# First feed-forward's end: where the residual rows of token tiles 4 to 7 are kept

## The chip, the cores and the metric

The program runs on one core of a Trainium2 chip. The metric is its time on the device in microseconds (us), from start to end of one execution, as the median of several runs. A core has five engines, each of which works through its own row of instructions in order: TensorE (PE, matrix products), VectorE (DVE), ScalarE (ACT), GpSimd (POOL) and SyncE (SP), which here only issues transfers. An instruction waits until what it reads has been written and until the buffer that it writes is no longer read, and all that stands behind it on its engine waits with it.

## The reference

One layer of a trunk over 1024 tokens of 1024 channels, in float32:

```python
x = x + 0.5 * rms_norm((silu(rms_norm(x) @ Wg) * (rms_norm(x) @ Wu)) @ W_out)   # first feed-forward, 2816 wide
u = rms_norm(x)
rq, rk, rv, rg, nq, nk, nv, g_ret, g_na = split(u @ w_mix_in)                   # one combined projection
y_ret = (silu(rg) * head_norm(forward + backward retention)) @ w_ret_out
y_na = neighbourhood_attention(nq, nk, nv, bias) @ w_na_out
x = x + rms_norm((sigmoid(g_ret) * y_ret + sigmoid(g_na) * y_na) @ w_mix_out)
x = x + 0.5 * rms_norm(second feed-forward of rms_norm(x))
```

Every norm has a gain of its own. The change lies where the first of these lines ends and the second and third begin.

## The kernel before, in words

**Products.** Each float32 product is made from operands split into a high and a low part (`wh` and `wl` for a block of weights): ACT rounds the high part (L61), DVE subtracts to get the low part (L62), and three matmuls, high by high (L88), high by low (L89) and low by high (L90), are summed in a bank of PSUM (`ps`, six banks, or `pt`, two). Large products are Strassen-like: operands are cut in quadrants a11, a12, a21, a22, sums s1 to s4 are formed, and seven products stand in place of eight.

**Raw blocks.** A block of weights, 512 KB, comes through `Core.raw` (L70): a buffer with the tag `wraw`, of which there are four in the whole program, and a transfer issued by SP (L72).

**The first feed-forward's end** is `ffn_out` (L674). It multiplies the 2816 gated channels of 1024 tokens by W_out. W_out lies in SBUF as four quadrants b11, b12, b21, b22 of three tiles each (`tiles[i][j]`; a tile holds four k-steps of 128 rows by 512 columns, and the third tile three). Seven products of eleven k-steps each run in the order a11, s1, s2, s3, a22, a12, s4, 77 steps in all. In a step the left factor, a block `g` of 512 KB, is loaded by SP (L625, from `g0a` for the product a12 and from `g0s` for s4), the right factor is a slice of a quadrant that is split into `wh` and `wl` (`x` in the names of the trace), and PE makes 4 x 3 matmuls of 128x512. POOL forms differences of quadrants ahead of use (t1 to t4): t4 reads b21 for the last product, and the product a12 reads b21 as its right factor. With that product b21 is spent, b11 and b12 are so earlier.

**The epilogue.** The products' ends (p1 to p7) combine seven results into the two halves of eight token tiles of 128 rows: tiles 0 to 3 are done with the product a22, tiles 4 to 7 with s4 (p3). For a token tile t, `Epilogue.steps` (L651) adds the normalised result to its residual rows, 512 KB that `xload(t)` has loaded (L659, DVE); stores the sum as x1 (L660, SP); squares it (L662, ACT); takes the reciprocal root (L98, POOL); and writes the normalised halves `q` (L670, DVE). Then `Core.flip` (L122) transposes them on PE (L127) and `Winograd.put` (L263) writes the mixing products' operand. For tiles 0 to 3 that is a split alone. For tiles 4 to 7 it is a longer chain: a copy of the transposed a21 (L278, ACT) and its store (L68, POOL), s3 (L282, L283, DVE), a22 (L61, L62), s1 (L288), s2 (L290, DVE), s4 (L293, L294, POOL), each split by ACT and DVE, s4's low part by POOL.

**What runs beside it.** While tiles 4 to 7 pass through, PE has other work from a filler: the neighbourhood values of token tiles 0 to 3 (`vproj`, with four blocks of value weights), and the first halves of three pairs of mixing products (`Pairs.leads`), each of which takes a raw block. Two of the value blocks are loaded and split in steps 65 and 66 (`side`). Behind the filler the first mixing pair's products run (L510 to L535 combine them and store `nq` and `nk`).

**What sets the order.** The program is written out once as a sequence; a scheduler then fixes each engine's row, by the sequence, by priorities, and by which buffers are free. A load goes into SP's row as early as its buffer is given free there. In `ffn_out`, the table `xloads` asks for the residual rows of tiles 4, 5 and 6 at steps 68, 69 and 70, and L775 for those of tile 7. The second feed-forward calls the same function with `ep.pre` None.

Of the kernel before, what the change touches and what calls it, by code (L numbers as in the profile page):

```python
# [673 lines left out]
def ffn_out(c, tiles, q, blocks, w_out, gl, ep, tail, side={}):  # L674
# [3 lines left out]
    nc = c.nc  # L678
# [3 lines left out]
    later, rest, flips, xs = [], [], [], {}  # L682
# [8 lines left out]

    def xload(t):

        if t < 4 or ep.pre is None:
            tile = (tiles[0][1] + tiles[0][0])[t // 2]
            xs[t] = tile[:, t % 2 * 2:t % 2 * 2 + 2].rearrange("p k f -> p (k f)")
            nc.sync.dma_start(xs[t], ep.resid(t))
        else:
            xs[t] = c.raw(ep.resid(t))


    order = []
# [31 lines left out]
    def p7(u, b):  # L734
        tt(q[3][:, u], b, q[1][:, u], ALU.add)

        def more():
            xload(u)
            add(q[1][:, u], q[1][:, u], q[2][:, u], ALU.add)
            add(q[2][:, u], q[3][:, u], q[2][:, u], ALU.add)  # L740
            ep.square(u, 1, q[2][:, u], spare[u])
        later.extend((more, None))
# [17 lines left out]
    def p3(u, b):  # L760
        e = tt(q[1][:, u], b, q[1][:, u], ALU.add)
        out = q[1][:, u] if ep.pre is not None else q[3][:, u]
        ep.square(4 + u, 1, q[1][:, u], b if ep.pre is not None else spare[2 + u % 2], out, nc.vector if u == 3 else nc.gpsimd)
        g = ep.steps(4 + u, xs[4 + u], (q[0][:, u], out))
        next(g)
        rest.append(g)
        if u > 0:
            with c.tc.issue_after(e.ins):
                next(rest[u - 1])
        if u == 3:  # L770
            next(g)
        if ep.pre is not None:
            flips.extend(next(rest[j]) for j in ((), (), (0,), (1, 2, 3))[u])
        if u == 2 and 7 not in xs:
            xload(7)  # L775
# [32 lines left out]
    for n, (i, k) in enumerate(steps):  # L808
        for m in range(2):
            operand(n + m)  # L810
        if n in loads:
            load(*loads[n])
        prepare(n)
        if n == NK:
            ep.gains()
        if n in side:
            side[n]()
        if n in xloads:
            xload(xloads[n])
        if later and i > 3:  # L820
            f = later.pop(0)
            if f:
                f()
        if k == 0:
            banks = {u: c.bank() if i % 2 == 0 or u < 2 else c.bank("pt", 2) for u in range(4)}
        ab = operands.pop(n)
        if i == len(products) - 1 and k >= NK - 4:
            last.append((k, *ab))
        else:
            for u in range(4):  # L830
                one(u, k, *ab)
        if k == NK - 1:
            operand(n + 2)
            for u in range(4):
                for e in last:
                    one(u, *e)
                products[i][2](u, banks[u])
# [755 lines left out]
```

## Time and profile before

| | us |
|---|---|
| runs | 2280.09, 2280.56, 2283.82 |
| median | 2280.56 |
| profiled execution | 2281.11 |
| its span | 2279.3 |
| PE busy | 2209.3 (97%) |
| DVE busy | 1662.9 (73%) |
| ACT busy | 1000.5 (44%) |
| POOL busy | 629.9 (28%) |

The times in the profile count from the start of the span. The page gives the busy time of each engine; the view of windows divides it into stretches; the view of waits says, for an engine and a stretch, which instruction waited for which; the timeline lists one engine's instructions with the idle time ahead of each in brackets and, behind the arrow, what ended it. L12 is line 12 of the kernel; names such as `wl<-wraw,wh` are what is written and what is read. SPq is SP's queue of transfers, of which only the issue is timed there.

### The profile page before, as it was taken

Reading aid. Unit: us, or ns where it says so; the run is one execution under the profiler, and the core shown is the slowest. Engines: PE = TensorE matmul, PEld = TensorE weight load, DVE = VectorE, ACT = ScalarE, POOL = GpSimd, SP = SyncE. Lnnn points to the kernel's source line nnn. Section 1 sums busy time; section 2 is a strip of 40 time slices with the busy share of each in tenths; the row PEclk is TensorE's granted clock in tenths of the full one; section 3 lists DMA queues with packets and bytes.
Section 4 is the critical chain, followed back from the end, with each engine's and each line's share of the span. In section 5 each row is a group of like instructions: output and inputs, shape, how many; then the busy total and the mean of one; then the engine's idle time right before and its main releaser. Section 6 shows DMA issues by size and latency. Waiting matters only on the chain. (4 is left out here: it accounts for less than half of the span.)

```text
span 2279.3 us, 30175 instructions
## 1 busy us (share of the span) xinstructions
PE 2209.3 (97%) x10232; PEld 1830.4 (80%) x10232; DVE 1662.9 (73%) x2928; ACT 1000.5 (44%) x2086; POOL 629.9 (28%) x779
## 2 busy tenths in 40 slices
PE   7899999999998999999999999999899999999998
PEld 5678888888786887878888888887678888888886
DVE  7898878755568657769876678537988787876444
ACT  5444434332344222349875665315644343433232
POOL 1121212168424122301101222101522121115942
PEclk9999999999999999999999999999999999999999
DMA  6354434598654564557745566866535444449865
GB/s 249 134 184 145 175 130 175 197 378 293 201 178 157 176 184 128 150 174 256 218 165 165 166 217 235 292 215 208 169 134 177 161 156 158 143 146 368 304 225 181
DMA packets 152650, 448.31 MB, mean 197 GB/s; under 512 B 19312, under 2 KB 47088, under 8 KB 150384
## 3 DMA queue, kind: packets, MB, share of 16 engines
q1 hardware_dynamic: 111216, 314.23, 41.1%
q0 software_dynamic: 41280, 132.15, 16.0%
q8 instruction: 81, 1.33, 0.2%
q14 instruction: 73, 0.60, 0.1%
HBM read 305.80 MB, written 144.70 MB: 198 GB/s over the span
## 5 line engine op out<-in xcount | busy, mean ns | idle before, releaser
L62 DVE TENSOR_TENSOR wl<-wraw,wh 128x512 fp32r<-128x512 f32 x512 | 353.3, 708 | 85.4 <-ACT wh L61 84.7
L61 ACT CAST wh<-wraw 128x512 fp32r<-128x512 f32 x516 | 297.6, 618 | 192.1 <-PE ps L89 63.2
L88 PE MATMUL ps<-wh,g 128*128 128x512 f32 x484 | 188.6, 390 | 0.0
L89 PE MATMUL ps<-wl,g 128*128 128x512 f32 x484 | 188.5, 390 | 0.0
L90 PE MATMUL ps<-wh,g 128*128 128x512 f32 x484 | 188.4, 389 | 0.0
L552 ACT ACTIVATE c<-c 128x512 f32<-128x512 f32 x88 | 55.5, 632 | 204.3 <-DVE c L517 103.9
L62 DVE TENSOR_TENSOR wl<-w,wh 128x512 fp32r<-128x512 f32 x77 | 76.4, 1005 | 84.2 <-ACT wh L61 83.2
L62 DVE TENSOR_TENSOR wl<-x,wh 128x512 fp32r<-128x512 f32 x77 | 78.8, 1040 | 76.5 <-ACT wh L61 75.1
L88 PE MATMUL ps<-a11h,wh 128*128 128x512 f32 x276 | 111.6, 404 | 9.2 <-ACT wh L61 9.2
L61 ACT CAST wh<-t 128x512 fp32r<-128x512 f32 x58 | 36.0, 621 | 184.2 <-DVE t L511 184.2
L90 PE MATMUL ps<-a11h,wl 128*128 128x512 f32 x276 | 109.4, 397 | 2.6 <-DVE wl L62 2.4
L88 PE MATMUL ps<-a22h,wh 128*128 128x512 f32 x280 | 109.8, 392 | 0.0
L90 PE MATMUL ps<-a22h,wl 128*128 128x512 f32 x280 | 109.2, 390 | 0.6 <-DVE wl L62 0.6
L89 PE MATMUL ps<-a11l,wh 128*128 128x512 f32 x276 | 109.5, 397 | 0.1
L89 PE MATMUL ps<-a22l,wh 128*128 128x512 f32 x280 | 109.1, 390 | 0.0
L88 PE MATMUL ps<-a12h,wh 128*128 128x512 f32 x276 | 108.8, 394 | 0.3 <-ACT wh L61 0.3
L90 PE MATMUL ps<-a12h,wl 128*128 128x512 f32 x276 | 107.5, 390 | 0.0
L89 PE MATMUL ps<-a12l,wh 128*128 128x512 f32 x276 | 107.5, 389 | 0.0
L89 PEld LDWEIGHTS ps<-wl,g 128*128 128x128 f32 x484 | 90.9, 188 | 19.1 <-DVE wl L62 0.5
L90 PEld LDWEIGHTS ps<-wh,g 128*128 128x128 f32 x484 | 90.8, 188 | 19.0
L88 PEld LDWEIGHTS ps<-wh,g 128*128 128x128 f32 x484 | 90.9, 188 | 18.7
L88 PE MATMUL ps<-s2h,wh 128*128 128x512 f32 x232 | 91.8, 396 | 6.8 <-ACT wh L61 6.8
(433 smaller groups left out, 6443.8 us busy)
## 6 DMA issues: line engine op xcount, KB each, us to landing
wraw<-in_dram SPq DMA_DIRECT2D x218, 512.0 KB, 4.5
g<-g0s SPq DMA_DIRECT2D x44, 512.0 KB, 4.2
g<-g1s SPq DMA_DIRECT2D x44, 512.0 KB, 4.6
g<-g0a SPq DMA_DIRECT2D x33, 512.0 KB, 3.3
g<-g1a SPq DMA_DIRECT2D x33, 512.0 KB, 4.4
g0s<-gth POOLq DMA_DIRECT2D x44, 256.0 KB, 5.2
g0s<-cmb POOLq DMA_DIRECT2D x44, 256.0 KB, 3.7
g1s<-gth POOLq DMA_DIRECT2D x44, 256.0 KB, 4.9
```

The costliest lines, as they stand in the source:

```text
L61: self.done = [nc.scalar.copy(h, src).ins, (eng or nc.vector).tensor_tensor(l, src, hf, ALU.subtract).ins]
L62: (eng or nc.vector).tensor_tensor(l, src, hf, ALU.subtract).ins]
L88: mm(ps, a[0], b[0], start=start, stop=False)
L89: mm(ps, a[0], b[1], start=False, stop=False)
L90: mm(ps, a[1], b[0], start=False, stop=stop)
L552: nc.scalar.activation(gate[j], gate[j], AF.Silu)
```

## The change

Residual rows of tiles 4 to 7 no longer take a buffer of raw blocks. They are loaded into halves of the first two tiles of b21: `tiles[1][0][0]` for tiles 4 and 5, `tiles[1][0][1]` for 6 and 7. For tiles 0 to 3, and for the second feed-forward, the place is as before. Lines behind L700 have a number lower by three in the changed kernel.

```diff
     def xload(t):
 
-        if t < 4 or ep.pre is None:
-            tile = (tiles[0][1] + tiles[0][0])[t // 2]
-            xs[t] = tile[:, t % 2 * 2:t % 2 * 2 + 2].rearrange("p k f -> p (k f)")
-            nc.sync.dma_start(xs[t], ep.resid(t))
-        else:
-            xs[t] = c.raw(ep.resid(t))
+        tile = (tiles[0][1] + tiles[0][0] if t < 4 or ep.pre is None else (None, None, *tiles[1][0]))[t // 2]
+        xs[t] = tile[:, t % 2 * 2:t % 2 * 2 + 2].rearrange("p k f -> p (k f)")
+        nc.sync.dma_start(xs[t], ep.resid(t))
```

The scheduler's rows change with it. SP, from the block loads of the product a12 to the mixing products: before, with `g<-g0a` and `g<-g0s` the blocks, `x_91` the stored x1, and the four `wraw` loads of residual rows among the L72,

```order
L625 DMA g<-g0s_83 128x1024
L660 DMA x_91<-x 128x512
L625 DMA g<-g0s_83 128x1024
L72 DMA wraw<-in_dram 128x1024
L625 DMA g<-g0s_83 128x1024 x2
L72 DMA wraw<-in_dram 128x1024
L625 DMA g<-g0s_83 128x1024 x6
L660 DMA x_91<-wraw 128x512 x4
L72 DMA wraw<-in_dram 128x1024
L660 DMA x_91<-wraw 128x512 x4
L72 DMA wraw<-in_dram 128x1024 x7
L1344 DMA tab<-in_dram 128x512 x4
```

and now. First the piece among a12's block loads:

```order
L625 DMA g<-g0a_79 128x1024 x11
L625 DMA g<-g0a_78 128x1024
L696 DMA x<-in_dram 128x1024
L625 DMA g<-g0a_78 128x1024 x2
L696 DMA x<-in_dram 128x1024
L625 DMA g<-g0a_78 128x1024 x2
L696 DMA x<-in_dram 128x1024
L625 DMA g<-g0a_78 128x1024 x2
L696 DMA x<-in_dram 128x1024
L660 DMA x_91<-x 128x512 x2
```

Then the piece further on, at the same place as the one before:

```order
L660 DMA x_91<-x 128x512
L625 DMA g<-g0s_83 128x1024
L72 DMA wraw<-in_dram 128x1024
L625 DMA g<-g0s_83 128x1024 x2
L72 DMA wraw<-in_dram 128x1024
L625 DMA g<-g0s_83 128x1024 x6
L660 DMA x_91<-x 128x512 x6
L72 DMA wraw<-in_dram 128x1024
L660 DMA x_91<-x 128x512 x2
L72 DMA wraw<-in_dram 128x1024 x4
L1341 DMA tab<-in_dram 128x512 x4
```

Four loads of residual rows (L696) have moved up among a12's blocks. The two L72 ahead of the last six blocks were the residual rows of tiles 6 and 7 and are two lead blocks now. The L72 between the stores, which was a value block, is the third lead block, and the value blocks' loads have moved up to the first two's place, ahead of this piece.

PE, where the last part of `vproj` meets the transposes of tile 5: before,

```order
L90 MATMUL ps<-wh,a11l 128x512
L88 MATMUL ps<-wh,a12h 128x512 x2
L127 MATMUL pt<-ident,q 128x128 x4
L88 MATMUL ps<-wh,a12h 128x512 x2
L88 MATMUL ps<-a11h,wh 128x512
L89 MATMUL ps<-wl,a12h 128x512
L90 MATMUL ps<-wh,a12l 128x512
L89 MATMUL ps<-wl,a12h 128x512
L90 MATMUL ps<-wh,a12l 128x512
L127 MATMUL pt<-ident,q 128x128 x4
L89 MATMUL ps<-wl,a12h 128x512
```

and now:

```order
L90 MATMUL ps<-wh,a12l 128x512
L88 MATMUL ps<-wh,a12h 128x512
L89 MATMUL ps<-wl,a12h 128x512
L90 MATMUL ps<-wh,a12l 128x512
L127 MATMUL pt<-ident,q 128x128 x4
L88 MATMUL ps<-wh,a12h 128x512
L89 MATMUL ps<-wl,a12h 128x512
L90 MATMUL ps<-wh,a12l 128x512
L88 MATMUL ps<-wh,a12h 128x512
L127 MATMUL pt<-ident,q 128x128 x4
L89 MATMUL ps<-wl,a12h 128x512
```

Before, the matmuls with the high part (`a12h`) of the last block stood ahead of those with `wl`, and a lead's first matmul (`ps<-a11h,wh`) among them; now each group is in plain order, and the transposes' second half comes soon behind the first.

DVE, from the epilogue of tiles 5 to 7 to the first flip (numbers behind a name tell buffers apart; `wl` of `wraw` is a low part of a raw block): before,

```order
L666 TENSOR_SCALAR ss4_3996<-ss4_3996 128x1
L666 TENSOR_SCALAR ss4_3998<-ss4_3998 128x1
L659 SCALAR_TENSOR_TENSOR wraw_5709<-q_3979,rstd_5727,wraw_5709 128x512
L659 SCALAR_TENSOR_TENSOR wraw_5709<-q_3980,rstd_5727,wraw_5709 128x512
L670 SCALAR_TENSOR_TENSOR q_3979<-wraw_5531,rstd_5742,gain1_3984 128x512
L670 SCALAR_TENSOR_TENSOR q_3980<-wraw_5531,rstd_5742,gain1_3984 128x512
L670 SCALAR_TENSOR_TENSOR q_3979<-wraw_5556,rstd_5747,gain1_3984 128x512
L670 SCALAR_TENSOR_TENSOR q_3980<-wraw_5556,rstd_5747,gain1_3984 128x512
L666 TENSOR_SCALAR ss4_4000<-ss4_4000 128x1
L282 TENSOR_TENSOR cmb_5794<-a11h_5217,cmb_5793 128x512
L670 SCALAR_TENSOR_TENSOR q_3979<-wraw_5709,rstd_5752,gain1_3984 128x512
L670 SCALAR_TENSOR_TENSOR q_3980<-wraw_5709,rstd_5752,gain1_3984 128x512
```

and now:

```order
L62 TENSOR_TENSOR wl_5856<-wraw_5849,wh_5855 128x512
L659 SCALAR_TENSOR_TENSOR x_3974<-q_3979,rstd_5723,x_3974 128x512
L659 SCALAR_TENSOR_TENSOR x_3974<-q_3980,rstd_5723,x_3974 128x512
L670 SCALAR_TENSOR_TENSOR q_3979<-x_3973,rstd_5738,gain1_3984 128x512
L670 SCALAR_TENSOR_TENSOR q_3980<-x_3973,rstd_5738,gain1_3984 128x512
L666 TENSOR_SCALAR ss4_3998<-ss4_3998 128x1
L666 TENSOR_SCALAR ss4_4000<-ss4_4000 128x1
L62 TENSOR_TENSOR wl_5917<-wraw_5914,wh_5916 128x512
L670 SCALAR_TENSOR_TENSOR q_3979<-x_3974,rstd_5743,gain1_3984 128x512
L670 SCALAR_TENSOR_TENSOR q_3980<-x_3974,rstd_5743,gain1_3984 128x512
L670 SCALAR_TENSOR_TENSOR q_3979<-x_3974,rstd_5748,gain1_3984 128x512
L670 SCALAR_TENSOR_TENSOR q_3980<-x_3974,rstd_5748,gain1_3984 128x512
```

The low parts of raw blocks have moved ahead of, or among, the L659 and L670 of tiles 5 to 7, and tile 4's L282, which stood among the L670, is the row behind this piece. From tile 7's L282 on the row is the same in both.

## The prediction

> **What bounds the kernel now.** I read the page first: its share of busy time.
>
> ```profile
> span 2279.3 us, 30175 instructions
> PE 2209.3 (97%) x10232; PEld 1830.4 (80%) x10232; DVE 1662.9 (73%) x2928; ACT 1000.5 (44%) x2086; POOL 629.9 (28%) x779
> ```
>
> TensorE (PE) is busy 97% of the span, so a change is worth only what it takes from PE's idle 70 us, or from its clock. The change acts at the first feed-forward's end. There I read the table of windows over the place where the feed-forward hands over to the mixing products (columns: sum, PE, PEld, DVE, ACT, POOL, clock, DMA share, GB/s).
>
> ```profile
> 670.00:680.00 10.00, 10.00 (x50) 8.39 (x49) 8.00 (x16) 5.28 (x16) 4.41 (x6) 1.00 0.44 151
> 680.00:690.00 10.00, 6.68 (x32) 5.20 (x30) 9.10 (x16) 4.99 (x11) 2.97 (x5) 1.00 0.83 267
> 690.00:700.00 10.00, 8.79 (x33) 6.99 (x34) 7.55 (x11) 6.35 (x12) 5.26 (x4) 0.83 0.35 109
> 700.00:710.00 10.00, 9.22 (x46) 7.36 (x44) 10.00 (x14) 6.16 (x12) 6.76 (x8) 1.00 0.48 147
> 710.00:720.00 10.00, 9.27 (x43) 7.79 (x44) 10.00 (x12) 3.92 (x7) 5.26 (x4) 1.00 0.88 305
> 730.00:740.00 10.00, 7.62 (x28) 6.21 (x29) 8.40 (x14) 3.35 (x7) 0.66 (x2) 0.83 0.38 131
> ```
>
> PE has holes in 680 to 700 and in 730 to 740, and VectorE (DVE) has none at all from 700 to 720. The next two views say what the holes wait for: PE's waits from 672 to 745, and PE's timeline.
>
> ```profile
> PE ps L88 <- ACT wh L61: 4.5, 1, 4.5
> PE ps L88 <- DVE ev L520: 3.0, 1, 3.0
> PE pt L127 <- DVE cmb L290: 1.5, 2, 1.2
> ...
> 682.66 0.39 PE L89 MATMUL ps<-wl,a11h 128*128 128x512 f32 x1
> 682.89 0.39 PE L90 MATMUL ps<-wh,a11l 128*128 128x512 f32 x1
> ...
> 691.21 0.79 PE L88 MATMUL ps<-a11h,wh 128*128 128x512 f32 x1 [4.53 <-ACT wh L61]
> ...
> 693.51 1.01 PE L127 MATMUL pt<-ident,q 128*128 128x128 f32 x4
> ...
> 732.38 0.77 PE L88 MATMUL ps<-s1h,wh 128*128 128x512 f32 x1 [3.00 <-DVE ev L520]
> ```
>
> The first wait, 4.53 us, is for the split (high part, ScalarE, ACT) of a raw W block. Why that is late is seen in SyncE's (SP's) issues of loads and ACT's waits and timeline.
>
> ```profile
> 586.12 24.80 SPq L625 DMA_DIRECT2D g<-g0a  x10
> ...
> 631.91 0.45 SPq L72 DMA_DIRECT2D wraw<-in_dram  x1
> ...
> 669.55 5.13 SPq L660 DMA_DIRECT2D x<-wraw  x4
> 677.19 0.33 SPq L72 DMA_DIRECT2D wraw<-in_dram  x1
> 678.40 3.85 SPq L660 DMA_DIRECT2D x<-wraw  x4
> 683.30 4.30 SPq L72 DMA_DIRECT2D wraw<-in_dram  x3
> ...
> ACT wh L61 <- DMA wraw<-in_dram: 5.7, 3, 2.5
> ...
> 690.54 0.62 ACT L61 CAST wh<-wraw 128x512 fp32r<-128x512 f32 x1 [1.81 <-DMA wraw<-in_dram]
> ```
>
> The four buffers of raw blocks hold residual rows from 631.91 on (x6 there, x7 later; x4 and x5 sat there before), until those are normalised and stored. Only then, at 677.19 and 683.30, do the loads of the value weights' last two blocks and of the first lead block go out, and ACT waits 5.7 us for them. This is the wait that the change aims at. Whether its end moves the program is a question for DVE:
>
> ```profile
> 675.70 1.42 DVE L670 SCALAR_TENSOR_TENSOR q<-wraw,rstd,gain 128x512 f32<-128x512 f32 x2 [1.12 <-POOL rstd L98]
> ...
> 680.49 1.41 DVE L659 SCALAR_TENSOR_TENSOR wraw<-q,rstd,wraw 128x512 f32<-128x512 f32 x2 [0.39 <-POOL rstd L98]
> ...
> 685.79 1.41 DVE L670 SCALAR_TENSOR_TENSOR q<-wraw,rstd,gain 128x512 f32<-128x512 f32 x2 [0.51 <-POOL rstd L98]
> ...
> 689.52 0.68 DVE L62 TENSOR_TENSOR wl<-wraw,wh 128x512 fp32r<-128x512 f32 x1
> ...
> 691.71 0.69 DVE L62 TENSOR_TENSOR s1l<-cmb,s1h 128x512 fp32r<-128x512 f32 x1 [0.91 <-ACT s1h L61]
> ...
> 693.75 0.69 DVE L62 TENSOR_TENSOR s2l<-cmb,s2h 128x512 fp32r<-128x512 f32 x1 [0.75 <-ACT s2h L61]
> ...
> 714.61 1.77 DVE L282 TENSOR_TENSOR cmb<-a11h,cmb 128x512 f32<-128x512 f32 x1
> ...
> 721.95 0.67 DVE L517 TENSOR_TENSOR ev<-ps,ev 128x512 f32<-128x512 f32 x1
> ...
> 731.56 0.68 DVE L520 TENSOR_TENSOR ev<-ps,ev 128x512 f32<-128x512 f32 x1
> ```
>
> and, from POOL's (GpSimd's) and ACT's timelines:
>
> ```profile
> 714.22 1.62 POOL L294 TENSOR_TENSOR cmb<-cmb,a12l 128x512 f32<-128x512 f32 x1
> ...
> 722.92 0.58 POOL L68 DMA_DIRECT2D nq<-ev  x1 [5.05 <-DVE ev L517]
> ...
> 726.25 1.62 POOL L294 TENSOR_TENSOR cmb<-cmb,a12l 128x512 f32<-128x512 f32 x1
> ...
> 727.91 0.62 ACT L61 CAST s4h<-cmb 128x512 fp32r<-128x512 f32 x1 [2.82 <-POOL cmb L294]
> ```
>
> Read the last seven backward: PE's wait at 732.38 ends with DVE's L520 (731.56), which stands in DVE's row behind pieces that ACT splits after s4h (727.91), which waits for POOL's L294 of token tile 7 (726.25), which stands behind a store that waits for DVE's L517 (721.95). L517 follows, with no idle DVE, on tile 7's L282 (714.61). So the time at which PE gets on with the mixing products is set by when DVE reaches tile 7's L282; PE's holes before that are in DVE's shadow. From that L282 on, DVE's row is the same in both kernels, and after the second pair PE runs without holes, so a shift of this point is the gain.
>
> **The change part by part.** The sum is made against the profiled execution, 2281.11 us (span 2279.3 and 1.8 around it); the median of the runs is 2280.56, or 0.55 less, and I take the same difference off both.
>
> *The raw blocks' loads.* All four blocks of value weights now load together, two lead blocks where x6 and x7 loaded. No load is added. ACT's 5.7 us of waits for blocks go; so does PE's 4.53. On the path is only what DVE gains ahead of 714.61. Three of its splitting pieces (0.68 each, row 689.52) now stand ahead of or among the L659 and L670 of tiles 5 to 7, where DVE waited 1.12, 0.39 and 0.51 for POOL: they fill 0.68 + 0.39 + 0.51 = 1.58 us. Behind them the waits for ACT's s1h and s2h (0.91 and 0.75) followed on ACT's own late block (1.81 at 690.54); they go, 1.66. Sum: 3.24 us. Bounds: DVE's whole idle time from 670 to 700 is 2.00 + 0.90 + 2.45 = 5.35 us by the windows, the upper end while DVE sets the pace; the lower end is 0, if tile 4's L282, now behind three pieces and all L670s, hands the waits on to later flips. I take 3.2, since each of its terms has a row.
>
> *What is late next on PE.* PE's holes were 4.53, 3.00 and 1.5. If its end moves by 3.2, some 6 us of holes stay. I look for them at the transposes (L127): tile 5's second half now comes ahead in PE's row and waits for ACT's copy that frees the bank, tile 7's for DVE's L290. What is queued behind is PE's own value projection, needed by nobody before DVE is through, so it costs nothing while the holes are shorter than what DVE sets.
>
> *The clock.* After the holes of 4.53 and 3.00 the granted clock reads 0.83 in those windows; from 691.21 to 693.51 five matmuls take 2.30 us where the spacing of 682.66 and 682.89 gives 1.15. A hole of 1.2 left 1.00 (700 to 720). So the dip at 691 was worth 1.15 on PE, in the same shadow: nothing. The Trainium skill (TensorE: Matmul & The Clock Gate, Why this matters for your kernels) warns of gaps over about 3 us on PE. By that rule the first dip is gone if no new hole reaches 3 us, and were PE the bound the gain would be larger, as in the first rival; the trace agrees on which holes were followed by a dip.
>
> *The residual rows.* Four loads move to about 597 to 610 among SP's block loads, each waiting for the last reader of its half tile:
>
> ```profile
> 609.07 0.73 DVE L62 TENSOR_TENSOR wl<-x,wh 128x512 fp32r<-128x512 f32 x1
> ...
> g<-g0a SPq DMA_DIRECT2D x33, 512.0 KB, 3.3
> ```
>
> SP issues ten block loads in 24.80 us there, one in 2.5. Behind a waiting load, a block slips by up to two places, 5 us. The order puts a block seven steps of 12 matmuls (12 x 0.227 = 2.72 us) ahead of its use, 19 us; less 3.3 of landing and 5 of slip, 10.7 us are left. Cost 0, hidden by that lead; beyond it each us would be a us of PE. The residual rows themselves are wanted some 60 us later.
>
> *The flip's operands.* s4's tiles use the same space and wait for the stores of x4 to x7 (eight halves, issued from 669.55 to 682.25); tile 4's half of s4 is the last of its flip, after the transposes at 693.51. Cost 0, hidden by those 11 us.
>
> *Neighbourhood attention's start.* One load (keys) waits for a later PE matmul than before.
>
> ```profile
> 1006.31 0.41 SPq L879 DMA_DIRECT2D kraw<-nk  x1
> ```
>
> The queries right behind it waited for that matmul already and went out 0.5 us later, so the cost lies between 0 and 0.5; I take 0, as PE has other work queued.
>
> Sum: -3.2; profiled 2277.9, **2277.4** as a median. A difference within 0.2% (4.56 us: 2276.0 to 2285.1) is about what a measurement of this kernel can't tell from no change.
>
> **The rivals.** *PE was the bound.* Then 4.53 + 1.15 = 5.7 us go: 2274.9. For it: 4.53 is the one long wait there, and its cause goes. Against it: DVE's two full windows behind. With the 3.00 shrinking too, down to 2272.
>
> *Nothing comes of it.* DVE does the same pieces in another order; tile 4's flip starts later, and the waits for POOL and ACT reappear at tiles 5 to 7: 2280.6. For it: DVE is at 10.00 from 700 to 720. Against: 5.35 us idle ahead.
>
> *Slower: DVE and POOL collide more.* Beside a POOL instruction of 1.62 us (714.22), DVE's L282 at 714.61 took 1.77, not 0.68: 1.1 us lost. With flips drawn together and four pieces moved, eight more such meetings cost 8.7, less 3.2: +5.5, 2286.1. Three use up the gain, seven make it measurably slower. For it: POOL is busy over half of 690 to 720. Against it: the same number of POOL instructions stands there in both kernels. The Trainium skill (SBUF — State Buffer, SBUF: two separate sides) states that a DVE instruction with two SBUF inputs and a GpSimd one that reads SBUF lock each other out for a whole instruction. By that rule the row's 1.77 is the rest of POOL's instruction and then its own; the trace agrees, as 715.84 + 0.54 is 716.38.
>
> *The change doesn't act*, because the scheduler keeps the order: SP's row speaks against it, with four loads moved.
>
> **How the numbers follow.** Forecast case 0.44, of which 0.10 past 2276.0, since the bound is 5.35; PE the bound 0.24; nothing 0.14; no action 0.02; collisions 0.16. Faster by over 0.2%: 0.10 + 0.24 = 0.34; within: 0.34 + 0.14 + 0.02 = 0.50; slower: 0.16. The range goes from 2273.0 (most of the first rival) to 2283.5 (part of the collisions); some 0.05 lies below and 0.14 above.
>
> **What would show it.** Right: no wait of ACT for raw blocks between 670 and 700; the 4.53 gone, shorter holes at L127; tile 7's L282 on DVE near 711.4; holes of PE from 672 to 745 about 6 us in all. PE the bound: L282 before 709.5. Nothing: L282 near 714.6. Collisions: more DVE pieces over 1.1 us between 685 and 725. Wrong altogether: PE waiting for a block (g) between 600 and 640, or a hole near 1006.

## The result and the profile after

Over twenty runs each, the changed kernel's median is 2278.57 us (2272.93 to 2282.47), the kernel before's 2282.18 (2276.47 to 2285.86): a ratio of 0.9985, with a 95% interval of 0.9979 to 0.9991, so 3.4 us less (2.1 to 4.8); the medians themselves lie 3.6 apart. Timed again on another chip it was 0.9987 (0.9977 to 0.9998). The forecast was 3.2 us less; its 2277.4 counted from the three runs' 2280.56. The profiled execution has a span of 2277.5 us, before 2279.3.

The view of windows of the changed kernel (sum, PE, PEld, DVE, ACT, POOL, granted clock, DMA share, GB/s):

```profile
690.00:700.00 10.00, 7.99 (x32) 6.63 (x33) 9.79 (x15) 5.40 (x10) 3.85 (x4) 0.83 0.29 79
...
710.00:720.00 10.00, 9.35 (x36) 7.66 (x37) 9.35 (x13) 4.19 (x8) 5.01 (x4) 0.83 0.66 240
...
730.00:740.00 10.00, 10.00 (x46) 8.29 (x45) 9.19 (x15) 3.26 (x6) 1.85 (x4) 1.00 0.46 173
```

PE's waits of the same kernel from 672 to 745, and PE's timeline at the first product s1:

```profile
PE pt L127 <- ACT cmb L278: 3.4, 1, 3.4
PE pt L127 <- DVE cmb L290: 2.4, 1, 2.4
...
692.01 1.12 PE L127 MATMUL pt<-ident,q 128*128 128x128 f32 x4 [3.42 <-ACT cmb L278]
...
710.65 0.63 PE L127 MATMUL pt<-ident,q 128*128 128x128 f32 x4 [2.39 <-DVE cmb L290]
...
730.44 0.39 PE L88 MATMUL ps<-s1h,wh 128*128 128x512 f32 x1
```

The wait of 4.53 us for a raw block's split is gone, and so is the wait of 3.00 ahead of s1h. Two waits at transposes stand in their place. PE's holes fell from 9.04 us (4.53, 3.00, 1.23 and 0.28) to 5.81.

SP's timeline: where the residual rows and blocks are loaded, where the two lead blocks go out, and the first store of tile 4's x1, from which the intervals below are counted (669.55 before).

```profile
597.22 0.33 SPq L696 DMA_DIRECT2D x<-in_dram  x1
597.64 1.71 SPq L625 DMA_DIRECT2D g<-g0a  x2
599.46 0.37 SPq L696 DMA_DIRECT2D x<-in_dram  x1
...
604.40 0.33 SPq L696 DMA_DIRECT2D x<-in_dram  x1
...
610.40 0.33 SPq L696 DMA_DIRECT2D x<-in_dram  x1
...
632.68 0.42 SPq L72 DMA_DIRECT2D wraw<-in_dram  x1
...
638.10 0.33 SPq L72 DMA_DIRECT2D wraw<-in_dram  x1
...
670.08 10.71 SPq L660 DMA_DIRECT2D x<-x  x6
```

DVE's timeline in the changed kernel, at the rows that answer to those of the prediction:

```profile
672.40 1.41 DVE L659 SCALAR_TENSOR_TENSOR x<-q,rstd,x 128x512 f32<-128x512 f32 x2 [0.34 <-POOL rstd L98]
...
673.98 1.54 DVE L62 TENSOR_TENSOR wl<-wraw,wh 128x512 fp32r<-128x512 f32 x1
676.48 1.41 DVE L670 SCALAR_TENSOR_TENSOR q<-x,rstd,gain 128x512 f32<-128x512 f32 x2 [0.96 <-POOL rstd L98]
...
681.70 1.41 DVE L659 SCALAR_TENSOR_TENSOR x<-q,rstd,x 128x512 f32<-128x512 f32 x2 [0.44 <-POOL rstd L98]
...
685.73 1.41 DVE L670 SCALAR_TENSOR_TENSOR q<-x,rstd,gain 128x512 f32<-128x512 f32 x2 [0.45 <-POOL rstd L98]
687.60 1.41 DVE L670 SCALAR_TENSOR_TENSOR q<-x,rstd,gain 128x512 f32<-128x512 f32 x2 [0.46 <-POOL rstd L98]
...
693.74 0.68 DVE L62 TENSOR_TENSOR s1l<-cmb,s1h 128x512 fp32r<-128x512 f32 x1
...
695.23 0.69 DVE L62 TENSOR_TENSOR s2l<-cmb,s2h 128x512 fp32r<-128x512 f32 x1 [0.21 <-ACT s2h L61]
...
712.23 0.68 DVE L282 TENSOR_TENSOR cmb<-a11h,cmb 128x512 f32<-128x512 f32 x1
```

Tile 7's L282 starts at 712.23, 42.15 us behind the first store; before it was 714.61 - 669.55 = 45.06. So DVE reaches it 2.9 us sooner. In the second profile of the same kernel it was 41.94, 3.1 sooner.

L520, whose end released PE ahead of s1h in the kernel before, is read in both profiles of the changed kernel, the first on DVE alone (its s1h stands above, at 730.44), the second with PE's s1h behind it:

```profile
728.76 0.68 DVE L520 TENSOR_TENSOR ev<-ps,ev 128x512 f32<-128x512 f32 x1
```

```profile
727.92 0.68 DVE L520 TENSOR_TENSOR ev<-ps,ev 128x512 f32<-128x512 f32 x1
728.75 0.47 PE L88 MATMUL ps<-s1h,wh 128*128 128x512 f32 x1 [0.60 <-DVE ev L520]
```

In the kernel before, s1h starts 0.14 us behind L520's end, in the second profile of the changed one 0.15. In the first profile it starts 1.00 behind it: there PE came late by itself, since it ran at a lowered clock behind the hole at 710 (0.83 in the window from 710 to 720).

### The profile page after: what moved, and what is told of

Read it like the earlier page. It is cut to its first block, busy times and chain, and to the rows that moved or that the text cites. A ratio compares the mean times of both kernels' runs of the same rounds, so it can differ in the third digit from the quotient of the medians.

```text
span 2277.5 us, 30187 instructions
## 1 busy us (share of the span) xinstructions
PE 2209.6 (97%) x10232; PEld 1832.5 (80%) x10232; DVE 1662.4 (73%) x2928; ACT 1000.4 (44%) x2086; POOL 630.3 (28%) x779
```

## The experiments

Three intervals serve as measures, all from tile 4's first store: to the end of DVE's L520; to the first matmul of s1h in the first mixing pair; and to the matmul behind a wait of 2.4 us that PE has in every kernel near 870, in the pairs' products. The last two contain what a lowered clock costs PE on the way, and only the last what it costs behind s1h. "Whole" is the changed kernel, in its first profile and in a second one. Each row is a single execution, not all of them on the same chip, and the two of "whole" differ by 1 us at s1h, which is how finely these rows can be read.

| kernel | to L520's end | to s1h | to 870's matmul | holes of PE, 672 to 745 |
|---|---|---|---|---|
| before | 62.69 | 62.83 | 200.60 | 9.0 |
| whole | 59.36 | 60.36 | 196.64 | 5.8 |
| whole, second | 59.16 | 59.31 | 195.71 | 6.1 |
| before, DVE +4 | 63.32 | 65.42 | 201.70 | 8.5 |
| whole, DVE +4 | 60.89 | 62.72 | 199.00 | 7.5 |
| before, PE -16 | 62.22 | 62.37 | 198.74 | 8.8 |
| whole, PE -16 | 58.79 | 58.93 | 195.30 | 8.1 |
| tiles 4, 5 alone | 59.53 | 59.68 | 196.05 | 6.0 |
| tiles 4, 5, timed | 59.92 | 60.06 | 196.47 | 6.2 |
| tiles 6, 7 alone | 60.72 | 60.86 | 197.24 | 7.3 |
| s3 of tile 5 on POOL | 61.49 | 61.63 | 199.59 | 7.5 |
| s3 of tile 4 on POOL, filler 6 | 60.28 | 60.42 | 196.83 | 6.1 |

The distance from L520's end to s1h tells which engine set s1h. In nine rows it is 0.14 or 0.15 us, so PE stood ready or was held up for L520. In the other three (whole in its first profile, and the two with more work for DVE) it is 1.0 to 2.1, and PE came late by itself.

**More work for DVE, in both kernels.** The edit, the same in each:

```diff
-            eng.tensor_tensor(self.s3, h1, self.a21, ALU.subtract)
+            [eng.tensor_tensor(self.s3, h1, self.a21, ALU.subtract) for _ in range(5 if t == 7 and self.spill is not None else 1)]
```

In the kernel before:

> The kernel before, with four more DVE instructions for token tile 7: L282 is issued five times with the same result (4 x 0.60 = 2.4 us of DVE, up to 1.1 more for each that meets a POOL instruction). Counted is the interval from the first store of x1 of tile 4 (L660) to the first matmul of s1h in the first mixing pair: 62.83 us in the profile before (669.55 to 732.38), and to the first neighbourhood score (L909): 348.93. Theory D (DVE's way to the end of tile 7 sets PE's end, as in the prediction): both grow by 2.4 us or somewhat more. Rival P (PE's own row sets it, the holes being PE's only loss): by less than 0.5.

In the changed one:

> The same four DVE instructions in the changed kernel. The intervals there are 60.36 us (670.08 to 730.44) and 344.87. Theory D, unchanged by the change: both grow by 2.4 us or more. Theory B (the change has brought PE and DVE level: PE has no hole at s1h any more, DVE's L520 ends at 729.44 and PE comes at 730.44, so DVE has about 1 us in hand): by about 1.4. Rival P: 0.

Measured to s1h: 62.83 to 65.42, or +2.59, and 60.36 to 62.72, or +2.36 (+3.41 against the second profile). That is the size which theory D names, but the added work did not get there by L520: in both, L520 itself waits for PE, 1.18 and 0.50 us. What it made late is tile 7's L290, behind that ACT's s2h, and PE's first matmul of s2h. The rows of the kernel before with the added work, PE and DVE:

```profile
726.32 0.79 PE L88 MATMUL ps<-s2h,wh 128*128 128x512 f32 x1 [3.77 <-ACT s2h L61]
...
734.93 0.39 PE L88 MATMUL ps<-s1h,wh 128*128 128x512 f32 x1
```

```profile
732.14 0.69 DVE L520 TENSOR_TENSOR ev<-ps,ev 128x512 f32<-128x512 f32 x1 [1.18 <-PE ps L90]
```

The hole of 3.77 us stands in the place of the 3.00 ahead of s1h, and PE's holes are 8.5 us in all, not more than the 9.0 without the added work. The rest is the clock: 24 matmuls take 8.61 us from 726.32 to 734.93, where the changed kernel needs 5.44 (725.00 to 730.44). Those 3.2 us make up the +2.59 and more; near 870 the difference is 1.10, at the first neighbourhood score 1.67 (348.93 to 350.60). There D's 2.4 was missed.

In the changed kernel with the added work the new hole is this one:

```profile
PE ps L88 <- ACT s2h L61: 1.6, 1, 1.6
```

Its holes are 7.5 us against 5.8, so 1.7 of the +2.36 is waiting, near B's 1.4, though at s2h and not at L520. It is +2.36 at 870 and +4.26 at the score (344.87 to 349.13). In both kernels PE stops for work that was given to DVE, which speaks against P; how much of it reaches the end isn't shown in the kernel before.

**Less work for PE, in both kernels.** Sixteen matmuls of the third lead pair are left out:

```diff
-                    self.c.mm3(self.begun[i][j], [p[:, k * P:(k + 1) * P] for p in b], (ah[:, k], al[:, k]),
-                               k == 0, k == 3)
+                    (self.c.mm3 if i < 2 else lambda ps, w, x, start, stop: self.c.nc.tensor.matmul(ps, w[0], x[0], start=start, stop=stop))(
+                        self.begun[i][j], [p[:, k * P:(k + 1) * P] for p in b], (ah[:, k], al[:, k]), k == 0, k == 3)
```

> The kernel before with 16 matmuls of the third lead pair left out (its low parts, L89 and L90, so its sums are less exact): 16 x 0.227 = 3.6 us of PE's work away after the flips, all of DVE's and ACT's kept. Theory D: PE comes earlier and waits longer, interval to s1h shorter by 0 to 0.5 us. Rival P: shorter by 3.6.

> The changed kernel with the same 16 matmuls left out. Theory D: 0. Theory B (level): shorter by the 1 us that DVE has in hand, then a wait of PE ahead of s1h of 2 to 3 us. Rival P: shorter by 3.6, no wait.

Measured to s1h: before -0.46, where 3.6 us of PE's work had gone. PE's waits and its row, and DVE's L520:

```profile
PE ps L88 <- ACT wh L61: 6.8, 2, 4.1
...
722.29 0.79 PE L88 MATMUL ps<-s2h,wh 128*128 128x512 f32 x1 [2.73 <-ACT wh L61]
...
731.33 0.47 PE L88 MATMUL ps<-s1h,wh 128*128 128x512 f32 x1
```

```profile
730.50 0.68 DVE L520 TENSOR_TENSOR ev<-ps,ev 128x512 f32<-128x512 f32 x1
```

PE did not get its 3.6 us back as waits: its holes are 8.8 us, before 9.0. Behind the hole at s2h its matmuls ran at a lowered clock, which by the same count of 24 cost some 3.3 us. That DVE still sets the point is read from L520: s1h starts 0.15 us behind its end (731.18), so PE would have had to wait for it at any clock, and L520 came only 0.47 us sooner than in the kernel before.

In the changed kernel it is -1.43 against the first profile and -0.38 against the second. Its waits with 16 matmuls less, without the two at transposes:

```profile
PE ps L88 <- ACT wh L61: 0.9, 1, 0.9
PE ps L90 <- DVE wl L62: 0.9, 1, 0.9
PE ps L88 <- DVE ev L520: 0.4, 1, 0.4
```

Three new waits, 2.3 us in all, and s1h is again released by L520. Theory D (nothing) and theory B (1 us that DVE has in hand, then waits) can't be told apart: that 1 us is there only in the first profile, where a lowered clock held PE up, and in the second PE waits 0.60 for L520. So the change brought PE and DVE within about 1 us of each other, and the clock of an execution decides which of them comes last.

The whole times of these four single executions are 2285.68, 2283.87, 2281.67 and 2273.40 us, beside 2279.79 for the kernel before; with single runs of one kernel up to 10 us apart, they decide nothing.

**Half of the change.** In the first kernel tiles 6 and 7 still take raw buffers, in the second tiles 4 and 5:

```diff
     def xload(t):
 
+        if t in (6, 7) and ep.pre is not None:      # second kernel: t in (4, 5)
+            xs[t] = c.raw(ep.resid(t))
+            return
```

> Half of the change: only the residual rows of tiles 4 and 5 lie in b21, those of 6 and 7 still take two raw buffers. All four value blocks then load early, but the three lead blocks only after the last stores, at about 685. Interval from the first store of x1 of tile 4 to the first s1h matmul (62.83 us before, 60.36 changed). Theory V (the value blocks are what was late, so they alone bring the gain): 60.4. Theory L (a lead block that comes late makes the same hole one step further on): PE's hole for ACT's or DVE's part of a raw block comes back at a lead's first matmul, 62.3 to 63.3.

> The other half: only the residual rows of tiles 6 and 7 lie in b21; tiles 4 and 5 take the two raw buffers. The last two value blocks load where x6 and x7 did (about 632), the first lead block between the stores, the others behind them. Theory V: 60.4 us. Theory L: lead blocks come about 4 to 6 us later than in the changed kernel but earlier than with the other half, so between the two, 60.4 to 62.

SP's timeline with tiles 4 and 5 alone: the lead blocks go out at 684.46, behind all stores.

```profile
669.13 4.09 SPq L660 DMA_DIRECT2D x<-x  x4
678.23 3.86 SPq L660 DMA_DIRECT2D x<-wraw  x4
684.46 15.36 SPq L72 DMA_DIRECT2D wraw<-in_dram  x4
```

and PE's waits there, with the one at a lead:

```profile
PE ps L90 <- DVE wl L62: 1.4, 2, 0.9
PE ps L88 <- DVE ev L520: 1.0, 1, 1.0
...
706.76 0.50 PE L90 MATMUL ps<-a12h,wl 128*128 128x512 f32 x1 [0.89 <-DVE wl L62]
```

A hole at a lead's matmul did come, as L says, but of 0.89 us, and it costs nothing at s1h, where PE still waits 1.0 for L520: 59.68 us, as good as the whole change. With tiles 6 and 7 alone it was 60.86, in L's range and within a profile's noise of V's 60.4, which decides nothing. So V holds and L falls by the first half: what was worth something were the two value blocks that used to be loaded at 677.19 and 683.30. No gain shows from the lead blocks going out some 50 us sooner. The half was then timed beside the whole:

> The half change of tiles 4 and 5 again, timed beside the whole change on the same chip. By its look it reaches the mixing products 0.6 us earlier than the whole change (the matmul behind the wait in the pairs, 196.05 against 196.64 us from tile 4's first store). Theory V: ratio to the kernel before as the whole change's, 0.998 to 0.999, the two within 1 us of each other. Theory L: 2 us slower than the whole change.

> The whole change, beside it: ratio 0.9985 within 0.0006, as measured before.

The half: 0.9986 (0.9977 to 0.9995). The whole: 0.9987 (0.9977 to 0.9998). They can't be told apart.

**Work moved from DVE to POOL.** Two versions of the changed kernel that might have beaten it. The first:

```diff
     wx = Winograd(c, (x0pool, x1pool, spool), None, (4, 4, 2, 8, 8, 8, 8), d["a21"])
+    wx.s3_on_pool = (5,)
```

> The changed kernel, with tile 5's s3 (L282 and L283) made by POOL, not DVE: 2 x 0.60 us off DVE ahead of tile 7, 2 x 1.62 onto POOL, which is idle for half of this stretch. Theory D (DVE still holds up PE's transposes and the mixing pair): interval to s1h shorter by 0.5 to 1.2 us, time 0.5 to 1 us under the changed kernel's. Rival (POOL's longer instructions slow DVE's by as much, or tile 5's operands come late): 0 or longer by up to 1.

The second has `(4,)` there, and one number of the filler's table:

```diff
-FLIP_FILL = (8, 8, 8, 8, 2)
+FLIP_FILL = (8, 6, 8, 8, 2)
```

> The changed kernel with tile 4's s3 on POOL and two fewer matmul groups of the filler (6, not 8) ahead of tile 5's transposes. Theory D: DVE's 1.2 us go, and PE's holes at the transposes (3.4 and 2.4) shrink by as much: s1h 1 to 1.5 us earlier than in the changed kernel, time about 1 us less. Rival: the holes only move, 0.

Ratios to the kernel before: 0.9992 (0.9982 to 1.0003) and 0.9989 (0.9979 to 0.9998), neither better than the whole change's. The first shows why, in POOL's timeline and DVE's beside it:

```profile
691.26 1.38 POOL L282 TENSOR_TENSOR cmb<-a11h,cmb 128x512 f32<-128x512 f32 x1
692.72 1.62 POOL L283 TENSOR_TENSOR cmb<-cmb,a11l 128x512 f32<-128x512 f32 x1
...
692.01 1.18 DVE L62 TENSOR_TENSOR s1l<-cmb,s1h 128x512 fp32r<-128x512 f32 x1
...
693.71 1.17 DVE L62 TENSOR_TENSOR s2l<-cmb,s2h 128x512 fp32r<-128x512 f32 x1
```

Two DVE instructions that take 0.68 elsewhere took 1.18 beside POOL's two. Summed from tile 6's last addition to tile 7's L282, the time of DVE's TENSOR_TENSOR rows beyond 0.60 each and 0.08 a row is 4.9 us before, 5.0 in the changed kernel and 8.2 here. Two of DVE's instructions that combine the first pair's weights (L510, L511) had also moved ahead of L282, and 1.0 of the 8.2 is L511's, beside another POOL instruction. The rival "POOL's longer instructions slow DVE's" holds, at a higher price than it named: s1h came 1.3 us later than in the changed kernel's first profile, 2.3 later than in its second. In the second version the holes only moved (5.0 at one transpose), as its rival said.

## Why the prediction was right

*DVE sets the end.* Held, by L520's row: in the kernel before, in the second profile of the changed one and in both with less work for PE, s1h starts 0.14 or 0.15 us behind its end. Taking 3.6 us from PE moved L520 by 0.47 in the kernel before; the change moved it by 3.33, and by 3.53 in the second profile. The added DVE work is weaker evidence, since its +2.59 in the kernel before is a lowered clock. The rival that PE was the bound asked for L282 before 709.5, and 5.7 us; L282 stands at 712.23 and, in the second profile, at 711.38.

*The sum, 3.24 us at tile 7's L282.* Measured 2.9, and 3.1 in the second profile. The size is right, but one of its two terms isn't what it was said to be. The waits for ACT behind s1h and s2h (1.66) went as forecast: none, and 0.21, so 1.45. The other, that the value blocks' pieces would fill 1.58 us of DVE's waits for POOL, failed: those waits are 0.96, 0.44, 0.45 and 0.46, 2.31 us in place of 2.02. The first piece met POOL's L649 and took 1.54 us, POOL's reciprocal root came later, and DVE waited again. What stands in place of that term is spread out. From tile 6's last addition to tile 7's L282 (43.76 us before, 40.86 now, the same instructions), DVE's idle time fell by 1.81 in all, from 4.67 to 2.86, and one L659 that had met POOL went from 2.46 to 1.41, as rows show:

```profile
671.88 2.46 DVE L659 SCALAR_TENSOR_TENSOR wraw<-q,rstd,wraw 128x512 f32<-128x512 f32 x2 [0.34 <-POOL rstd L98]
```

is the row before; the one of the changed kernel stands above at 672.40. That a sum came out while a term did not is partly luck. ACT's waits for raw blocks from 670 to 700 are gone, as forecast.

Behind L282 the row of DVE is the same, as the prediction says, but not its time: to the start of L520 it takes 16.95 us before and 16.53 now. A wait of 2.35 for ACT (at 729.08 before) is gone, but DVE's instructions take longer there: L521 and L530, for example, took 0.68 each before and take 1.78 each now, beside POOL. So the 2.9 at L282 became 3.3 at L520.

*New holes at the transposes, some 6 us of holes in all.* Held: 3.42 for ACT's copy at tile 5 and 2.39 for DVE's L290, 5.81 us in all. The second was said to be tile 7's; by its place in PE's row it is.

*The clock at no price.* This is the step that was mis-sized. The dip at 691 lies in DVE's shadow, as was said. The one behind the last hole does not, and the sum left it out: after 732.38 PE was the bound, and it ran slowly until 735.08.

```profile
735.08 0.50 PE L88 MATMUL ps<-s1h,wh 128*128 128x512 f32 x1
735.42 0.39 PE L89 MATMUL ps<-s1l,wh 128*128 128x512 f32 x1
```

Six matmuls took 2.70 us, at 0.227 each 1.36: 1.34 lost. In the changed kernel no hole and no dip stand there. The sum also left out that a new hole can bring a dip of its own: the one behind the hole at 710.65 is why s1h gained only 2.47 us in the first profile, where L520 gained 3.33. In the second profile, with no dip there, s1h gained 3.52. To 870's matmul the gain is 3.96 (200.60 to 196.64). Of that 3.23 are holes, the rest, 0.73, matmuls at a lowered clock; in the second profile it is 4.89, of which 2.9 and 2.0. The median's 3.4 (2.1 to 4.8) can't separate 3.2 from 4. The prediction also says that PE has no holes behind the second pair; there is the one of 2.39 near 870, in both kernels.

*Blocks and residual rows at no cost.* Held. The residual rows' loads stood at 597.22, 599.46, 604.40 and 610.40. Counted from tile 4's first store, the block behind the first of them went out 5.1 us later than before, the two places that the prediction allowed, and PE waited for none: its one hole from 600 to 640, 1.6 us at transposes, is in both kernels, and 620 to 680 reads 10.00 in both.

*Neighbourhood attention's start.* Held, in the changed kernel's SP timeline:

```profile
1002.85 0.42 SPq L876 DMA_DIRECT2D kraw<-nk  x1
```

The keys' load is 332.77 us behind tile 4's first store, before 1006.31 - 669.55 = 336.76: 4.0 sooner, as all else there.

*Collisions.* The slower rival's mechanism is real, as the version with s3 on POOL shows, but up to tile 7's L282 the change did not add to it (4.9 and 5.0 us). By the sign that the prediction named there are more: ten DVE pieces over 1.1 us from 685 to 725, before eight, L521 and L530 among the ten. One sum of that rival is short: seven meetings less 3.2 come to 4.4 us, still inside its bound of 4.56; it takes eight.

## What to carry to other kernels

A hole of the busiest engine is worth what the next engine in line can give back: here 4.53 us of PE's waiting went, and 2.5 to 3.5 came out at the mixing products, because DVE could come 3.3 us sooner. To see which engine sets a point, look how far the released instruction starts behind the end of its releaser, in the kernel as it is and with work taken from the released engine. A shift alone can mislead: split it into holes and matmuls at a lowered clock first, since here +2.59 us had the forecast size and another cause. When buffers are short, ask which of the late loads matters: half of this change, two of the four buffers, can't be told from the whole.

## What the runs showed of the hardware that was not expected

A hole of the same length is followed by a lowered clock in some executions and not in others. In the kernel before, the wait near 870 left the clock at 1.00; in the changed kernel with 16 matmuls less, the same wait at 862.95 did not. First before, then that kernel, PE's row and the window of the clock:

```profile
870.15 0.50 PE L90 MATMUL ps<-a11h,wl 128*128 128x512 f32 x1 [2.39 <-DVE wl L62]
...
870.00:880.00 10.00, 9.85 (x43) 7.92 (x44) 8.28 (x14) 4.96 (x9) 3.66 (x5) 1.00 0.69 136
```

```profile
862.95 0.50 PE L90 MATMUL ps<-a11h,wl 128*128 128x512 f32 x1 [2.38 <-DVE wl L62]
...
860.00:870.00 10.00, 7.62 (x27) 5.78 (x26) 8.89 (x14) 4.43 (x8) 6.15 (x8) 0.83 0.60 109
```

Of the twelve profiles five have the dip there (the second of the whole change, and the four with DVE's or PE's work changed); the hole was 2.38 or 2.39 in all. A dip costs about 1.5 us, by an estimate from the second window: PE's 7.62 us hold 27 matmuls there, and at 0.227 each there is room for some 33. Likewise the hole of 2.39 at 710 of the changed kernel was followed by 0.83 in its first profile, one of 2.38 with 16 matmuls less by 1.00. Every hole of 2.7 us or more between 672 and 745 had a dip at it or behind it, and one of 1.63 with 0.23 close behind (the changed kernel with more work for DVE, 724.75) had one too.

In windows of 1 us the changed kernel's clock reads 0.53, 0.50, 0.50 and 0.76 from 712 to 716, so this lowered stretch lasts about 3.4 us. By the same reading it starts at 712.06, and the one before at 691.58: 20.48 us apart, six times 3.41. The two of the kernel before lie 40.96 apart, twelve times as much. The Trainium skill (TensorE: Matmul & The Clock Gate, What's actually happening) says that the clock gate watches activity in a free-running window, so that the moment in the window counts; the runs agree with that. They don't agree with a fixed length of a hole: one of 2.39 us is under the 3 us that the prediction quotes, and at times it was enough. The phase may be part of why single executions of one kernel lie several us apart; how large a part was not measured.
